# Sums of squares by TensorE, roots from products with ones and full-height low keys in a two-layer hybrid decoder step

## The chip, the core and the metric

The kernel runs on one core of a Trainium2 chip. A core has TensorE (PE, matrix products into PSUM), VectorE (DVE), ScalarE (ACT, functions from a table), GpSimd (POOL) and SyncE (SP, which here only issues DMAs); every engine works through its own queue in order. The metric is the time of one execution on the device in microseconds (us), median of several runs.

## What is computed

Two layers of a decoder step on a prompt of 1024 tokens and on 8 sequences of 4 new tokens; all 1056 tokens (T) share the weights. Cut to what matters here:

```python
mod = silu(c) @ w_ada + b_ada                     # shift, scale, gate
h = rms(x, g_pre) * (1 + scale) + shift           # rms: x * rsqrt(mean(x*x) + EPS) * g
u_a, bch, glu, q, k, v, mgate, mrg = split(h @ w_in)
y_a = pool_mixer(u_a); y_b = b_g * dwconv3(c_g * h_b)
y_c = silu(layernorm(dwconv31(val * sigmoid(gl))))
p = softmax(q k / 8) ; w = p[0] - lam * p[1]      # two maps per head, 64 deep each
y_d = rms(w @ v, g_subln) * (1 - lam_init)
merged = sum_n sigmoid(mrg_n) * (y_n * silu(mgate_n)) @ w_branch_n
x = x + gate * rms(merged @ w_o, g_post)
```

## The kernel before

Activations lie with channels on the 128 partitions and tokens along the row, in three column blocks `b` of TB = 352 tokens; the last 32 columns of block 2 are the sample tokens. Each product of float32 matrices is made of three products of rounded halves: `hh` and `hl` are the high and low part of the normed input, `whi` and `wlo` those of a weight tile, and `gemm` (line 238) issues `whi*hh`, `wlo*hh`, `whi*hl` for 8 slices `k` of 128 channels. A unit is 128 output channels: 24 products of 128x352 for each block. `drive` walks through the units, calls an evaluation function for each result, and between products it steps a second stream of work (`side`): the attention of a head (`attn`), the sample attention (`decode`) or the LayerNorm.

**Head.** Before the first unit, the program loads the input blocks `x0`, `x1`, `x2` (1408 KB each), the modulation weights `wa` (four slices `n` of four tiles, 512 KB each) and the first three weight tiles. `ada_first(n)` multiplies a slice with silu(c) (line 300), copies the result, transposes it (314) and adds the bias; slices 2 and 0 give scale and shift for the first four `k`, slices 3 and 1 for the others. `sumsq` (372 to 374) squares the input on ACT in two halves and adds the squares up on DVE; `rstd_x` makes the reciprocal root of it and broadcasts it to all partitions. `norm_apply` (L396 to L398) then makes `hh` and `hl`; for `k` in NORM_POOL it runs on POOL (391 to 394). The first products of blocks 0 and 1 use only `k` 0 to 3 (HALVES).

**Roots.** `rstd_of` sums over the partitions with products whose right side is one column of ones (349), so that the sums land on the partitions; ACT takes the square root (351), DVE the reciprocal (352), splits it in two rounded parts (355, 356) and writes each as a diagonal matrix (360); products with `ones` broadcast them (364). It is called twice at the end of each head's attention, 4 times by `decode`, 6 times by the LayerNorm, for each block behind the output projection, and for the next layer's input.

**Scores.** `a_part(qb)` makes the scores of 128 queries for one head: for each of the two maps `j` the products with the high keys and the mask, and then, for both maps together, the products with the low keys `kl`: map 0's low keys lie on partitions 0 to 63, map 1's on 64 to 127, and the products use 64 rows each.

A scheduler orders the instructions of every engine but SP from the order of the code and its own durations; SP's loads stand in the order of the code.

## Time and profile before

| what | us |
|---|---|
| median of 3 runs | 3004.43 (3002.55 to 3007.85) |
| profiled execution: its own time | 3002.23 |
| profiled execution: span of the core | 3000.4 |
| TensorE busy | 2913.8, 97% of the span |
| VectorE, ScalarE, GpSimd busy | 1634.2, 970.6, 495.1 |

The span is the profile's clock from the first to the last instruction; 1.8 us of the execution's own time lie outside it. Busy time of TensorE counts the time until a product has left the array, so that products overlap; what a product costs in a stream is the distance from its start to the start of the next one. The profile also gives the clock that was granted to TensorE: 1.0 is 2.4 GHz, 0.5 is 1.2 GHz.

### The profile page before, as it was taken

To read this page: it belongs to the slowest core of one execution; us is meant where nothing else is said; L and a number is where in the kernel's file an instruction comes from. 1 tells how busy PE (TensorE), PEld (TensorE's weight loads), DVE (VectorE), ACT (ScalarE), POOL (GpSimd) and SP (SyncE) were. 2 spreads that over 40 slices of the span, in tenths; PEclk is the share of its full clock that TensorE was granted. 3 is DMA by queue.
4 is the path that set the end of the run, shared out by engine and by line. 5 is a ranking of instruction groups with operands and counts; after the bars stand their busy time and mean duration, and the time that the engine had idled before them with its cause. 6 is when DMAs were issued, how large, how long until landed. Compare 5 with 4: busy or idle time off the path is not lost.

```text
span 3000.4 us, 46185 instructions
## 1 busy us (share of the span) xinstructions
PE 2913.8 (97%) x18436; PEld 2781.6 (93%) x18436; DVE 1634.2 (54%) x2540; ACT 970.6 (32%) x1904; POOL 495.1 (17%) x642
## 2 busy tenths in 40 slices
PE   6999999999999999999989999999999999999998
PEld 4899889989999999999989998998899999999998
DVE  7756356577972145323487663664889522543233
ACT  4544245313112123212454551542221121322132
POOL 3221011012200111011230120101140001110123
PEclk8999999999999999999999999999999999999999
DMA  6122621362233223222321236115511221221122
GB/s 230 48 65 85 203 78 53 116 196 64 67 109 105 80 86 96 97 75 71 108 98 48 67 118 205 49 45 153 179 38 59 84 76 43 80 90 57 50 69 97
DMA packets 135961, 280.08 MB, mean 93 GB/s; under 512 B 18338, under 2 KB 88994, under 8 KB 134210
## 3 DMA queue, kind: packets, MB, share of 16 engines
q10 hardware_dynamic: 45072, 145.74, 15.9%
q1 hardware_dynamic: 79778, 90.73, 9.7%
q0 software_dynamic: 10896, 40.67, 3.6%
q8 instruction: 145, 2.38, 0.3%
q14 instruction: 70, 0.57, 0.1%
HBM read 240.73 MB, written 36.34 MB: 92 GB/s over the span
## 4 chain that ended last, share of the span: by engine, by line
PE 84%; DVE 7%; DMA 2%; issue 2%; SPq 2%; ACT 2%; POOL 0%; DVEq 0%; ACTq 0%; POOLq 0%
PE mm_t L238 45%; PE m_t L238 28%; PE s_t L238 3%; PE ms_t L238 2%; DVE acc_t L954 2%; SPq L671 1%; PE ms_t L611 1%; PE s_t L776 1%; DVE wlo_t L211 1%; PE s_t L702 1%; DVE acc_t L373 1%; DMA e_t<-in_kc_dram 1%; PE ms_t L349 1%; PE b_t L238 1%; ACT rop_t L497 1%
## 5 line engine op out<-in xcount | busy, mean ns | idle before, releaser
L238 PE MATMUL mm_t<-hh_t,whi_t 128*128 128x352 f32 x2792 | 533.3, 329 | 5.8 <-ACT hh_t L385 2.1
L238 PE MATMUL mm_t<-hh_t,wlo_t 128*128 128x352 f32 x2792 | 528.6, 327 | 0.0
L238 PE MATMUL mm_t<-hl_t,whi_t 128*128 128x352 f32 x2792 | 524.0, 325 | 0.0
L211 DVE TENSOR_TENSOR wlo_t<-wst_t,whi_t 128x1024 fp32r<-128x1024 f32 x203 | 268.5, 1329 | 455.6 <-ACT whi_t L210 455.4
L238 PEld LDWEIGHTS mm_t<-hh_t,whi_t 128*128 128x128 f32 x2792 | 458.7, 190 | 27.6 <-issue 14.6
L238 PEld LDWEIGHTS mm_t<-hh_t,wlo_t 128*128 128x128 f32 x2792 | 460.5, 189 | 9.7 <-issue 8.2
L238 PEld LDWEIGHTS mm_t<-hl_t,whi_t 128*128 128x128 f32 x2792 | 458.7, 189 | 6.7 <-issue 5.6
L954 DVE SCALAR_TENSOR_TENSOR acc_t<-uc_t,vec_t,acc_t 128x1024 f32<-128x1024 f32 x240 | 320.4, 1360 | 1.6
L1164 POOL TENSOR_TENSOR mg_t<-mg_t,th_t 128x352 f32<-128x352 f32 x144 | 144.7, 1008 | 925.8 <-DVE th_t L1163 925.7
L210 ACT ACTIVATE whi_t<-wst_t 128x1024 fp32r<-128x1024 f32 x203 | 213.3, 1056 | 246.7 <-PE mm_t L238 163.6
L238 PE MATMUL m_t<-hh_t,wlo_t 128*128 128x352 f32 x1352 | 249.7, 325 | 0.0
L238 PE MATMUL m_t<-hl_t,whi_t 128*128 128x352 f32 x1352 | 247.6, 324 | 0.0
L238 PE MATMUL m_t<-hh_t,whi_t 128*128 128x352 f32 x1352 | 246.4, 323 | 0.0
L238 PEld LDWEIGHTS m_t<-hh_t,wlo_t 128*128 128x128 f32 x1352 | 223.6, 190 | 0.9
L238 PEld LDWEIGHTS m_t<-hl_t,whi_t 128*128 128x128 f32 x1352 | 222.7, 189 | 0.0
L238 PEld LDWEIGHTS m_t<-hh_t,whi_t 128*128 128x128 f32 x1352 | 222.0, 189 | 0.1
L1072 ACT ACTIVATE th_t<-m_t 128x352 f32<-128x352 f32 x114 | 52.6, 463 | 373.4 <-PE m_t L238 362.5
L1072 ACT ACTIVATE th_t<-mm_t 128x352 f32<-128x352 f32 x78 | 35.9, 463 | 272.0 <-PE mm_t L238 240.9
L590 DVE TENSOR_REDUCE sml_t<-s_t 128x1 f32<-128x256 f32 (+7 forms) x128 | 92.4, 752 | 53.1 <-PE s_t L238 52.7
L593 ACT ACTIVATE e_t<-s_t,sml_t 128x256 f32<-128x256 f32 (+7 forms) x128 | 94.3, 744 | 69.7 <-DVE sml_t L591 39.9
L238 PE MATMUL m_t<-yh_t,whi_t 128*128 128x352 f32 x460 | 94.5, 326 | 0.0
L238 PE MATMUL m_t<-yh_t,wlo_t 128*128 128x352 f32 x460 | 93.1, 324 | 0.0
(349 smaller groups left out, 3854.0 us busy)
## 6 DMA issues: line engine op xcount, KB each, us to landing
wst_t<-in_wst_dram ACTq DMA_DIRECT2D x209, 512.0 KB, 3.6
e_t<-in_kc_dram SPq DMA_DIRECT2D x224, 128.0 KB, 3.0
e_t<-in_vc_dram SPq DMA_DIRECT2D x216, 128.0 KB, 2.6
rld_t<-ysp_t ACTq DMA_DIRECT2D x16, 528.0 KB, 4.5
wa_t<-in_wada_dram SPq DMA_DIRECT2D x16, 512.0 KB, 10.4
wlo_t<-in_wada_dram ACTq DMA_DIRECT2D x16, 512.0 KB, 3.7
whi_t<-in_wada_dram ACTq DMA_DIRECT2D x16, 512.0 KB, 4.3
x_t<-in_xT_dram SPq DMA_DIRECT2D x3, 1408.0 KB, 6.0
```

Of the source, the lines that this page charges most:

```text
L210: sc.activation(out=R(hi), in_=st, func=AF.Copy)
L211: (eng or ve).tensor_tensor(out=R(lo), in0=st, in1=hi, op=ALU.subtract)
L238: last_mm[0] = m = te.matmul(out=out, lhsT=R(lh), rhs=R(rh), start=first and i == 0, stop=last and i == n - 1)
L349: te.matmul(out=pc[:, j:j + 1], lhsT=x[:, j * w:(j + 1) * w], rhs=ones[:, 0:1], start=True, stop=True)
L373: ve.tensor_reduce(out=acc[:, i], in_=o.rearrange("p k n -> p n k"), axis=AX.X, op=ALU.add)
L497: sc.activation(out=sw[32 * (g ^ 1):32 * (g ^ 1) + 32], in_=pb[32 * g:32 * g + 32], func=AF.Copy)
L590: ve.tensor_reduce(out=s[:, j:j + 1], in_=S[j][:, :n], axis=AX.X, op=ALU.max)
L593: sc.activation(out=E[qb % 2][j][:, :n], in_=S[j][:, :n], func=AF.Exp, bias=s[:, 2 + j:3 + j], scale=0.125, accum_out=s[:, 4 + j:5 + j])
L611: te.transpose(out=pb[:, k], in_=e0[:, (k0 + k) * P:(k0 + k + 1) * P], identity=ident)
L954: pace(ve.scalar_tensor_tensor(out=a, in0=v, scalar=w(k), in1=a, op0=ALU.mult, op1=ALU.add))
L1072: sc.activation(out=th[:, b * TB:(b + 1) * TB], in_=pb, func=AF.Tanh, scale=0.5)
L1164: gp.tensor_tensor(out=mg[:, d, cl], in0=mg[:, d, cl], in1=th, op=ALU.add)
```

## The change

Of the head: the order of loads becomes `x0`, slices 0 and 2, the weight tiles, `x1`, slices 1 and 3, `x2` (before `x0`, `x1`, slices 0 and 2, weight tiles, `x2`, slices 1 and 3). The sums of squares are no longer added on DVE: eight float32 products with `ones` (128x352 each) add the squares up and broadcast them in one step. POOL has no part in the modulation of the first layer any more, except for the sample columns. Block 1's first half now comes before slices 1 and 3.

Of the roots: `rstd_of` splits its input in two rounded parts (ACT, DVE), two products with `ones` sum and broadcast it, and ACT and DVE then make the reciprocal root on all columns, with one correction step (4 operations on 128 x 352 or 512 elements). The factor -2 that the correction leaves is put into constants and into the operations that use the root.

Of the scores: the queries of a block are copied into `qz` with zeros in the other 64 rows (two copies on ACT), so that the products with the low keys use all 128 rows; they follow the high keys of their own map, and the pairing of the two maps falls away.

```diff
-    def rstd_of(x, n, scale, dg, pb=None):
-        w = max(w_ for w_ in (P, TB // 4, 64) if n % w_ == 0)
-        m = n // w
-        pc = ms(m)[:w]
-        for j in range(m):
-            te.matmul(out=pc[:, j:j + 1], lhsT=x[:, j * w:(j + 1) * w], rhs=ones[:, 0:1], start=True, stop=True)
-        r = const("rsm", 8, bufs=2)[:w, 0:m]
-        sc.activation(out=r, in_=pc, func=AF.Sqrt, bias=epsc[:w], scale=scale)
-        ve.reciprocal(out=r, in_=r)
...
-        for i, d in enumerate(dg):
-            te.matmul(out=pb, lhsT=cast(ones[:w]), rhs=cast(d[:w]), start=i == 0, stop=i == len(dg) - 1)
+    def rstd_of(x, scale, parts, yt, pb=None):
+        if parts:
+            hi, lo = parts
+            sc.activation(out=R(hi), in_=x, func=AF.Copy, scale=scale)
+            ve.scalar_tensor_tensor(out=R(lo), in0=x, scalar=scale, in1=hi, op0=ALU.mult, op1=ALU.subtract)
+            for i in range(2):
+                te.matmul(out=pb, lhsT=R(ones), rhs=R(parts[i]), start=i == 0, stop=i == 1)
+        else:
+            te.matmul(out=pb, lhsT=ones, rhs=x, start=True, stop=True)
...
+        sc.activation(out=y, in_=pb, func=AF.Abs_reciprocal_sqrt, bias=epsc)
+        sc.activation(out=t, in_=y, func=AF.Square)
+        ve.scalar_tensor_tensor(out=pb, in0=pb, scalar=EPS, in1=t, op0=ALU.add, op1=ALU.mult)
+        ve.scalar_tensor_tensor(out=pb, in0=pb, scalar=-3.0, in1=y, op0=ALU.add, op1=ALU.mult)
...
                 for j in range(2):
-                    for c0, w in chunks:
-                        c = slice(c0, c0 + max(w, 256))
+                    r = slice(64 * j, 64 * j + 64)
+                    sc.activation(out=R(qz[r, qb % 2, j]), in_=qs[j][r, q1], func=AF.Copy)
+                for j in range(2):
+                    for c in chunks:
                         gemm(S[j][:, c], [(qs[j][:, q1], ks[j][:, c])], last=False)
-                    gemm(S[j][:, q1], [(identr, maskr)], first=False, last=False)
+                        if c is chunks[-1]:
+                            gemm(S[j][:, q1], [(identr, maskr)], first=False, last=False)
+                        gemm(S[j][:, c], [(qz[:, qb % 2, j], kl[:, c])], first=False)
                     if j == 0:
                         yield
-                hi = last_mm[0]
-                for c0, w in chunks:
-                    c = slice(c0, c0 + max(w, 256))
-                    for j in range(2):
-                        r = slice(64 * j, 64 * j + 64)
-                        gemm(S[j][:, c], [(qs[j][r, q1], kl[r, c])], first=False, on=hi)
...
         def rstd_x(b):
-            a = accs[b]
-            pb = rstd_of(a[:, 0], TB, 1.0 / D, [a[:, 1]])
-            sc.activation(out=a[:, 0], in_=pb, func=AF.Copy)
-        for b in range(2):
-            sp.dma_start(out=xb0[b], in_=xT[b])
+            t, y = two(accs[b])
+            pb = ms(TB)
+            for i in range(2):
+                tx = su("tx", 4, TB, bufs=2)
+                sc.activation(out=tx, in_=xb0[b][:, 4 * i:4 * i + 4], func=AF.Square)
+                for k in range(4):
+                    te.matmul(out=pb, lhsT=ones, rhs=tx[:, k], start=i + k == 0, stop=i + k == 4)
...
+        sp.dma_start(out=xb0[0], in_=xT[0])
...
+        sp.dma_start(out=xb0[1], in_=xT[1])
         ada_first(2, psA("mm", 512))
...
+        first_half(0)
+        rstd_x(1)
+        first_half(1)
+        for n in (1, 3):
+            ada_first(n, ms())
+        make_A(0, 4, 4)
+        rstd_x(2)
```

How this moves the instructions on TensorE, at three places. `cs_t` holds the identity of a transpose, `m_t` a copied modulation slice, `tx_t` the squared input, `acc_t` the sums before.

The first instructions of TensorE, before:

```order
L300 MATMUL mm_t<-wa_t,scs_t 32x512 x8
L314 MATMUL ms_t<-cs_t,m_t 128x128 x4
L349 MATMUL ms_t<-ones_t,acc_t 88x1 x4
L300 MATMUL mm_t<-wa_t,scs_t 32x512 x4
L364 MATMUL ms_t<-acc_t,ones_t 128x352
L349 MATMUL ms_t<-ones_t,acc_t 88x1 x4
L300 MATMUL mm_t<-wa_t,scs_t 32x512 x4
L364 MATMUL ms_t<-acc_t,ones_t 128x352
L314 MATMUL ms_t<-cs_t,m_t 128x128 x4
L238 MATMUL b_t<-hh_t,whi_t 128x352 x3
```

and now:

```order
L1260 MATMUL ms_t<-tx_t,ones_t 128x352 x4
L298 MATMUL mm_t<-wa_t,scs_t 32x512 x2
L1260 MATMUL ms_t<-tx_t,ones_t 128x352 x4
L298 MATMUL mm_t<-wa_t,scs_t 32x512 x10
L312 MATMUL ms_t<-cs_t,m_t 128x128 x4
L298 MATMUL mm_t<-wa_t,scs_t 32x512 x4
L312 MATMUL ms_t<-cs_t,m_t 128x128 x4
```

The eight products for block 0's squares now stand ahead of almost all modulation products, and the root of block 1 is gone from the place ahead of the first unit.

The end of the first head's attention on TensorE (from the last products with the values, `vl_t`, to the last product with `ones`), before:

```order
L238 MATMUL ms_t<-e_t,vl_t 128x256
L349 MATMUL ms_t<-ones_t,ms_t 128x1 x4
L238 MATMUL mm_t<-hh_t,whi_t 128x352 x6
L238 MATMUL mm_t<-hh_t,wlo_t 128x352 x8
L238 MATMUL mm_t<-hl_t,whi_t 128x352 x8
L238 MATMUL mm_t<-hh_t,whi_t 128x352 x8
L364 MATMUL ms_t<-e_t,ones_t 128x512
L349 MATMUL ms_t<-ones_t,ms_t 128x1 x2
L364 MATMUL ms_t<-e_t,ones_t 128x512
L349 MATMUL ms_t<-ones_t,ms_t 128x1 x2
L238 MATMUL mm_t<-hh_t,wlo_t 128x352 x8
```

and now:

```order
L236 MATMUL ms_t<-e_t,vl_t 128x256
L236 MATMUL mm_t<-hh_t,wlo_t 128x352
L236 MATMUL mm_t<-hl_t,whi_t 128x352 x8
L236 MATMUL mm_t<-hh_t,whi_t 128x352 x6
L354 MATMUL ms_t<-e_t,ones_t 128x512
L236 MATMUL mm_t<-hh_t,whi_t 128x352 x2
L236 MATMUL mm_t<-hh_t,wlo_t 128x352 x3
L354 MATMUL ms_t<-e_t,ones_t 128x512
L236 MATMUL mm_t<-hh_t,wlo_t 128x352 x5
L236 MATMUL mm_t<-hl_t,whi_t 128x352 x5
L354 MATMUL ms_t<-e_t,ones_t 128x512
```

The one-column products are gone; between the last products with the values and the first product with `ones` stand 15 products of units.

The scores of a block of 768 keys on TensorE, first head before (`kl_t` the low keys, `maskr_t` the mask):

```order
L238 MATMUL s_t<-k_t,q_t 128x512
L238 MATMUL s_t<-k_t,q_t 128x256
L238 MATMUL s_t<-maskr_t,identr_t 128x128
L238 MATMUL mm_t<-hh_t,whi_t 128x352 x2
L238 MATMUL s_t<-k_t,q_t 128x512
L238 MATMUL s_t<-k_t,q_t 128x256
L238 MATMUL s_t<-maskr_t,identr_t 128x128
L238 MATMUL s_t<-kl_t,q_t 128x512 x2
L238 MATMUL s_t<-kl_t,q_t 128x256 x2
```

and now, third head (`ms_t` is the tile of `qz`):

```order
L236 MATMUL s_t<-k_t,q_t 128x512
L236 MATMUL s_t<-kl_t,ms_t 128x512
L236 MATMUL s_t<-k_t,q_t 128x256
L236 MATMUL s_t<-maskr_t,identr_t 128x128
L236 MATMUL s_t<-kl_t,ms_t 128x256
L236 MATMUL s_t<-k_t,q_t 128x512
L236 MATMUL s_t<-kl_t,ms_t 128x512
L236 MATMUL s_t<-k_t,q_t 128x256
L236 MATMUL s_t<-maskr_t,identr_t 128x128
L236 MATMUL s_t<-kl_t,ms_t 128x256
```

Each map's low keys have moved up to its own high keys, chunk by chunk, ahead of the other map's products.

## Rows read from the trace of the kernel before

**Rows 1.** The page, part 1: busy us, share of the span, instructions.

```profile
PE 2913.8 (97%) x18436; PEld 2781.6 (93%) x18436; DVE 1634.2 (54%) x2540; ACT 970.6 (32%) x1904; POOL 495.1 (17%) x642
```

**Rows 2.** The page, part 4: the chain that ended last, by engine.

```profile
PE 84%; DVE 7%; DMA 2%; issue 2%; SPq 2%; ACT 2%; POOL 0%; DVEq 0%; ACTq 0%; POOLq 0%
```

**Rows 3.** Chain of the first 80 us, in order: start, us, what.

```profile
1.21 5.97 DMA x_t<-in_xT_dram
...
8.61 2.55 DVE acc_t L373
...
36.46 1.25 PE b_t L238 x3
```

**Rows 4.** Stretches: us; engines' busy time (instructions); PEclk, DMA share, GB/s.

```profile
20.00:36.00 16.00, 10.78 (x44) 5.73 (x44) 11.64 (x24) 7.29 (x12) 4.28 (x5) 0.53 1.02 412
...
78.00:82.00 4.00, 3.56 (x13) 3.56 (x14) 2.98 (x8) 2.64 (x5) 3.97 (x13) 0.50 0.12 45
```

**Rows 5.** Timeline, TensorE, head: start, us, line, out<-in, shape, [idle before <-who].

```profile
25.40 1.51 PE L364 MATMUL ms_t<-acc_t,ones_t 88*128 88x352 f32 x2 [0.27 <-DVE acc_t L360]
26.70 1.24 PE L349 MATMUL ms_t<-ones_t,acc_t 128*88 128x1 f32 x8
...
29.84 1.51 PE L364 MATMUL ms_t<-acc_t,ones_t 88*128 88x352 f32 x2
...
51.76 1.92 PE L300 MATMUL ms_t<-wa_t,scs_t 128*32 128x512 f32 x16
...
60.45 0.76 PE L364 MATMUL ms_t<-acc_t,ones_t 88*128 88x352 f32 x2
...
78.44 0.90 PE L526 MATMUL ms_t<-cs_t,vcm_t 128*128 128x128 f32 x3 [6.07 <-ACT vcm_t L541]
```

**Rows 6.** Timeline, ScalarE: first and last of the chain ahead of 78.44.

```profile
68.26 0.92 ACT L497 ACTIVATE rop_t<-b_t 32x352 f32<-32x352 f32 x2
...
77.92 0.46 ACT L541 ACTIVATE vcm_t<-mm_t 128x352 f32<-128x352 f32 x1
```

**Rows 7.** Groups of VectorE: modulation with GpSimd beside it, and without (layer 1).

```profile
L396 DVE SCALAR_TENSOR_TENSOR x_t<-x_t,Am_t,acc_t 128x352 f32<-128x352 f32 x12 | 8.5, 768 | 0.0
...
L396 DVE SCALAR_TENSOR_TENSOR ob_t<-xb_t,Am_t,ms_t 128x352 f32<-128x352 f32 x16 | 8.1, 577 | 7.0 <-PE ms_t L364 7.0
```

**Rows 8.** One-column products: timeline of one call, then groups from 100 us on.

```profile
162.70 0.95 PE L349 MATMUL ms_t<-ones_t,ms_t 128*128 128x1 f32 x8
163.51 1.22 PE L238 MATMUL mm_t<-hh_t,whi_t 128*128 128x352 f32 x6
...
L349 PE MATMUL ms_t<-ones_t,ms_t x128: 164/250/250, 162.7 to 2053.1; 128*128 128x1 f32 x128
L349 PE MATMUL ms_t<-ones_t,ls_t x48: 164/217/217, 1105.0 to 2655.3; 128*88 128x1 f32 x48
```

**Rows 9.** Timeline, TensorE: scores of a block of 1024 and of 256 keys.

```profile
252.63 0.63 PE L238 MATMUL s_t<-k_t,q_t 128*128 128x512 f32 x2
253.10 0.22 PE L238 MATMUL s_t<-maskr_t,identr_t 128*128 128x128 f32 x1
253.25 0.73 PE L238 MATMUL s_t<-kl_t,q_t 64*128 64x512 f32 x4
253.91 0.51 PE L238 MATMUL ms_t<-e_t,vh_t 128*128 128x256 f32 x2
...
201.41 0.38 PE L238 MATMUL s_t<-kl_t,q_t 64*128 64x256 f32 x2
201.73 0.76 PE L238 MATMUL mm_t<-hh_t,whi_t 128*128 128x352 f32 x3
```

**Rows 10.** Timeline of the end: the last root.

```profile
2985.74 0.52 DVE L1211 TENSOR_TENSOR ssq_t<-ssq_t,sq_t 128x352 f32<-128x352 f32 x1
2986.32 0.79 PE L349 MATMUL ms_t<-ones_t,ssq_t 128*88 128x1 f32 x8 [1.69 <-DVE ssq_t L1211]
...
2989.62 0.89 DVE L1219 TENSOR_TENSOR ob_t<-ob_t,ada_t 128x704 f32<-128x704 f32 x1 [0.75 <-PE ada_t L364]
```

More of the change, by code (lines that the diff above doesn't have):

```diff
@@ L375, in sumsq, with norm_apply @@
         return acc[:, 0]
-    def norm_apply(l, b, x, t, rs, hh, hl, pool=(), ks=range(KC)):
+    def norm_apply(l, b, x, t, rs, hh, hl, ks=range(KC)):
         n = npr(b)
@@ L644, in attn @@
                 c = slice(i * 512, i * 512 + 512)
-                dg = ep(f"e{i}", 1024)
-                rs = rstd_of(msq[:, c], 512, 1.0 / P, two(dg.rearrange("p (i n) -> p i n", i=2)))
+                dg, yt = [ep(f"e{i + x}", 1024).rearrange("p (i n) -> p i n", i=2) for x in (0, 2)]
+                msq = ep(f"e{4 + i}", 1024)[:, 0:512]
+                sc.activation(out=msq, in_=o[:, c], func=AF.Square)
+                rs = rstd_of(msq, 1.0 / P, two(dg), two(yt))
                 ve.tensor_tensor(out=o[:, c], in0=o[:, c], in1=rs, op=ALU.mult)
@@ L1096, in layernorm @@
                 yield from skip(6)
-                rs = rstd_of(s2, TB, 1.0 / 512, [lnp("ls1", TB), lnp("ls3", TB)])
-                ve.tensor_tensor(out=x, in0=x, in1=rs.unsqueeze(1).to_broadcast([P, 4, TB]), op=ALU.mult)
+                rs = rstd_of(s2, 1.0 / 512, [lnp(f"lr{i}", TB) for i in range(2)], [t[:, i] for i in range(2)])
+                ve.scalar_tensor_tensor(out=x, in0=rs.unsqueeze(1).to_broadcast([P, 4, TB]), scalar=-0.5, in1=x,
+                                        op0=ALU.mult, op1=ALU.mult)
                 for c in range(4):
@@ L1215, in layer @@
                 ve.tensor_tensor(out=scols(ob[:, :, n:]), in0=scols(ob[:, :, n:]), in1=samp(GG), op=ALU.mult)
-            rs = rstd_of(ssq, TB, 1.0 / D, two(op("acc", 2, TB)), psM("ada", 512)[:, 0:TB])
+            rs = rstd_of(ssq, 1.0 / D, two(op("parts", 2, TB)), two(op("yt", 2, TB)), psM("ada", 512)[:, 0:TB])
             for d in range(0, KC, 2):
                 o_, x_ = ob[:, d:d + 2], xb[:, d:d + 2]
-                ve.tensor_tensor(out=o_, in0=o_, in1=rs.unsqueeze(1).to_broadcast([P, 2, TB]), op=ALU.mult)
+                ve.scalar_tensor_tensor(out=o_, in0=rs.unsqueeze(1).to_broadcast([P, 2, TB]), scalar=-0.5, in1=o_,
+                                        op0=ALU.mult, op1=ALU.mult)
                 (gp if d % 4 else ve).tensor_tensor(out=x_, in0=x_, in1=o_, op=ALU.add)
@@ L1222, in layer @@
                 gp.dma_start(out=xmid[b], in_=xb)
-                rs = rstd_of(sumsq(xb, ob, op("acc", 2, TB)), TB, 1.0 / D, two(op("acc", 2, TB)))
+                rs = rstd_of(sumsq(xb, ob, op("acc", 2, TB)), 1.0 / D, two(op("parts", 2, TB)), two(op("yt", 2, TB)))
                 for t, x in zip(nh, "hl"):
```

69 lines of the change are left out of this document (26 added, 43 removed).

## The prediction

> **What bounds the kernel now.** I read the page first: TensorE is busy for 97% of the span, no other engine for more than 54% [rows 1], and 84% of the chain that ended last is TensorE's own work [rows 2]. So what counts is what leaves TensorE's queue, and the few places where that queue stands still. The chain of the first 80 us shows the largest of them, the head: the first unit product starts at 36.46 [rows 3], behind a chain of squares on ACT and sums on DVE. In the timeline there is one more wait of 6.07 us that ends at 78.44 [rows 5]. Loads are no shorter than this: between 20 and 36 us the DMA engines are full, at 412 GB/s [rows 4].
>
> **The head.** Block 0 of the input lands at 1.21 + 5.97 = 7.2 and its first square is done at 8.6 [rows 3]. Removed are the sums on DVE (six of 2.55, the first in [rows 3]) that paced the squares; added are eight float32 products for each block. Their price has two ends. At a granted clock of 0.5 such a product takes 26.70 - 25.40 = 1.30; at full clock it is half, 0.65, as its busy time shows (1.51 against 0.76) [rows 5]. The granted clock was 0.53 between 20 and 36 [rows 4], where TensorE had waits between short products. The new queue begins with full-height products of 352 columns one behind the other from 8.6 on; I take the full clock from some 15 us on, and keep the half clock as a rival.
>
> Slice 2 decides when the first unit can start. x1 (1408 KB, 1.44 MB) now lies behind it: 3.5 us at 412 GB/s. By bytes (x0 at 7.2, then 6.0 MB) slice 2 landed at 21.9 and now lands at 18.4. By then TensorE has done block 0's eight products (some 8.6 to 16, slice 0 between them, part of it at half clock) and gets through slice 2 at 20.8. Before, 36.46 - 31.14 = 5.3 passed from the end of the last root products (29.84 + 1.30) [rows 5] to the first unit product [rows 3]. With the copy ahead of it (0.6) that gives 20.8 + 0.6 + 5.3 = 26.7. That POOL no longer works beside DVE makes a modulation 577 instead of 768 ns [rows 7], against two more for each half block: a wash, taken as nothing.
>
> From there on everything is in TensorE's queue. A product of 352 columns costs 0.162, since 1024 columns took 253.10 - 252.63 = 0.47 [rows 9]. Half of block 0 is 36 of them, 5.9, and 6.4 as DVE has to write the low parts: 33.1. Block 1's eight: 5.2, 38.3. Slices 1 and 3 land by then; their 16 products cost 2 x 1.92 [rows 5] and 0.6 for transposes: 42.7. Half of block 1: 48.6. Transposes 0.6 and block 2's eight, 5.2: 54.4. Block 2 itself lands last of all loads, near 40, and waits for nobody. The first unit of block 0 is finished after 38 further products: 60.6. Then TensorE runs into the wait that it has today: ScalarE needs from 68.26 to 78.38 to take away the units and to make block 2's high parts [rows 6], 10.1 us, and the change leaves that list as long as it was. So the wait ends at 70.7 instead of 78.4: **-7.5**. The bound on the good side is -9, with full clock from the first product. If half clock holds until the first unit product, this starts at 32.8, the following pieces move with it, and the wait ends near 79.7: +1.3.
>
> **The roots.** A call of `rstd_of` loses its one-column products: eight records at the end of attention cost TensorE 163.51 - 162.70 = 0.81 [rows 8]. The products with `ones` that broadcast stay, two for each call, with the same columns. Per layer there are 8 calls in attention, so 16: -13.0. With 88 instead of 128 columns of weights a call is put at 88/128 of that, 0.56; 15 such calls lie behind the head: 6 of the LayerNorm (48 records of eight a call [rows 8]), 6 behind the output projection, 3 for the next layer's input. Three of them end in a wait of TensorE for the chain anyway (the last of all, two at the layer boundary), so 12: -6.7. Four calls of the sample attention have two records each: -0.8. Sum **-20.5**, all of it in stretches where TensorE is the bound.
>
> What is added lies on ACT and DVE: for each call a copy, a root and a square on ACT and three operations on DVE, on 352 or 512 columns, instead of short ones on 4 columns and two diagonals. That is nothing where TensorE has other products queued: 15 of them (2.4 us) stand between the last products with the values and the first with `ones`. At two places there is no cover. At the end, before: from 2986.32 to 2989.62, 3.3 [rows 10]. Now a copy 0.46, a difference 0.52, the products 0.6, root and square 2 x 0.46, two corrections 2 x 0.52, and some 0.3 between them: 3.9 (0.46 is a 352-column copy on ACT [rows 6], 0.52 a 352-column operation on DVE [rows 10]). **+0.6**, and **+0.6** again at the layer boundary, where the first unit of block 2 waits for the second root.
>
> The root now also keeps one of the two PSUM tiles of its kind for some 4 us longer, and table loads on ACT fall into that time; transposes of the next head need such a tile. Today TensorE does not wait there; I take 0, and up to 1.5 for each of the 8 heads, +12, for the range.
>
> **The low keys.** Before, a block of 1024 keys occupies TensorE from the mask at 253.10 to the next product at 253.91, 0.81, of which the mask's 128 columns are 0.06: 0.75. With all rows in use it is 2 x 0.47 = 0.94 [rows 9]. For 256 keys it was 253.25 - 253.10 - 0.06 + 201.73 - 201.41 = 0.41, and will be 2 x 0.12. So the paired products do run beside each other, but each time 0.3 is lost when they begin and end. Over the eight blocks of a head (256 twice, 384, 512, 768 twice, 896, 1024 columns, 4864 in all, the middle ones by the same two parts) it is 4.53 before and 4864 x 0.47 / 1024 = 4.47 after: **-0.5** for 8 heads.
>
> The Trainium skill speaks against this edit: "TensorEngine Tiling (Array Packing)", Theoretical Speedup, promises a speedup where a contraction of at most 64 rows is packed as several tiles that work at once. By that rule alone the edit gives up the whole gain of the pairs, 17.9 in all as in rival 3. The row for 256 keys speaks against it: 0.41 is more than the 0.24 of the single file.
>
> The two copies of queries for each block are 128 instructions on ACT, at about 0.3 each 35 us of an engine that is 32% busy; in ACT's order they stand right behind the queries' own split, well ahead of the scores. Taken as 0. Decode's first cache loads wait for the root's tiles; the second diagonal came late (its column sums stood behind the first root), now both halves run closer together, while two more tiles are held a little longer. Taken as 0, with -6 as the bound.
>
> **The sum.** -7.5 - 20.5 + 0.6 + 0.6 - 0.5 = -27.3. From the profiled execution's 3002.2 this is 2974.9; that execution lay 2.2 under the median of 3004.4, so I predict 2977.
>
> **Rivals.** (1) *Half clock in the head*: +1.3 instead of -7.5, 2986. For it: 0.53 between 20 and 36 with TensorE two thirds busy [rows 4]; against: those were products of 32 or one column. Chance 0.17. (2) *Roots become waits*: PSUM tiles or table loads stop TensorE at the heads' ends, +12: 2989. Against: half of ACT and DVE is free. 0.12. (3) *The loss at entry and exit stays*: if the 0.3 per block belongs to the change between high and low keys and not to the pairs, the new form has it too, and a head gives up half of its 4.47, 2.24; for 8 heads that is +17.9 in place of -0.5: 2977 + 18.4 = 2995. For it: no product with low keys on 128 rows is in the trace; against: high keys follow each other without such a loss [rows 9]. 0.06. (4) *Slower*: TensorE waits at each product with low keys for the copy of the queries, because ACT has it behind an exponential or an evacuation. 128 such products, each behind one ACT operation of 0.46 [rows 6] and the wait for it, 0.5 together: +64, 3041. It decides from 27.3 / 128 = 0.21 per product on. Against it: queries are ready long before, and two blocks are held. 0.03. That the edit of the column sums does not take place is out: the one-column products are gone from the order.
>
> **How the numbers follow.** The forecast's own case has 0.62 and spans 2964 to 2984 (from -6 for the loads, -1.5 for the head and a part of the waits, to some waits). The range of 2962 to 2989 takes in the first two rivals. A measurement of this kernel tells about 0.2%, 6 us, from no change. Faster by more: 0.62 + 0.17 + 0.12 + most of 0.06, 0.94; within: 0.03; slower: 0.03.
>
> **What would show it.** Head right: TensorE's first unit product near 26.7, the wait for ScalarE ends near 71; wrong: PEclk 0.5 up to the first unit product, or a new wait at slices 1 and 3. Roots right: no group of one-column products, and the LayerNorm and output stretches shorter by 0.56 for each call; wrong: waits of TensorE for the root's tiles at heads' ends. Low keys right: scores as long as before within 1 us a head, no wait for the copies. End right: 0.6 longer from the last sum to the first multiplication.

## The result

| kernel | median, us | range | runs |
|---|---|---|---|
| before | 3003.49 | 3001.87 to 3007.85 | 4 |
| changed | 2973.56 | 2970.82 to 2977.08 | 4 |

The ratio is 0.9899, with a 95% interval of 0.9882 to 0.9916: 29.9 us less, where the prediction had 2977 and a range of 2962 to 2989. The profiled execution of the changed kernel took 2971.34, its span is 2969.6, against 3000.4 before.

### The profile after

The page of the changed kernel, parts 1 and 4 (as [rows 1, 2]):

```profile
PE 2882.3 (97%) x18198; PEld 2774.0 (93%) x18198; DVE 1618.5 (55%) x2488; ACT 1060.0 (36%) x2086; POOL 483.1 (16%) x632
...
PE 80%; DVE 7%; ACT 5%; DMA 3%; SPq 3%; issue 2%; POOL 0%; ACTq 0%; DVEq 0%; POOLq 0%
```

TensorE is the bound as before. 238 products less were recorded; ScalarE is busy for 89 us more and has grown from 2% to 5% of the chain that ended last. That is the first hint of what the list of waits shows (changed kernel, TensorE; columns: product and line, waited for, us in total, times, longest):

```profile
PE s_t L236 <- ACT e_t L585: 11.3, 8, 3.2
PE ms_t L236 <- ACT dh_t L1014: 9.4, 2, 5.3
...
PE ms_t L354 <- ACT parts_t L351: 7.9, 2, 7.7
PE mm_t L236 <- ACT hh_t L383: 4.8, 1, 4.8
PE ms_t L518 <- ACT vcm_t L533: 4.4, 1, 4.4
...
PE ada_t L354 <- ACT parts_t L351: 2.2, 1, 2.2
PE ms_t L1084 <- DVE ls_t L1081: 2.0, 3, 1.1
```

The first row is new: at eight places score products wait for exponentials. The waits of decode for its cache loads fell from 12.9 to 8.0 (the two stretches of `decode` in the lists of both kernels).

Places of the program that both kernels have, with their starts in the two timelines, split the gain into stages. The last column is the prediction's sum for the stage.

| up to | before | changed | stage | predicted |
|---|---|---|---|---|
| first score product | 84.40 | 78.01 | -6.4 | -7.5 |
| first merge step of layer 1 on GpSimd (`mg_t`) | 964.45 | 948.54 | -9.5 | -7.2 |
| first product with `woh_t`, layer 1 | 1439.49 | 1420.80 | -2.8 | -1.7 |
| first merge step of layer 2 | 2445.45 | 2416.10 | -10.7 | -8.8 |
| first product with `woh_t`, layer 2 | 2900.82 | 2871.56 | +0.1 | -1.7 |
| end of the span | 3000.4 | 2969.6 | -1.5 | -0.5 |

The sum is close, -30.8 against -27.4, but two stages with attention won more than forecast although they have a new wait. So some terms must be wrong in both directions.

### The profile page after: what moved, and what is told of

Read it like the earlier page. It is cut to its first block, busy times and chain, and to the rows that moved or that the text cites. A ratio compares the mean times of both kernels' runs of the same rounds, so it can differ in the third digit from the quotient of the medians.

```text
span 2969.6 us, 45889 instructions
## 1 busy us (share of the span) xinstructions
PE 2882.3 (97%) x18198; PEld 2774.0 (93%) x18198; DVE 1618.5 (55%) x2488; ACT 1060.0 (36%) x2086; POOL 483.1 (16%) x632
## 4 chain that ended last, share of the span: by engine, by line
PE 80%; DVE 7%; ACT 5%; DMA 3%; SPq 3%; issue 2%; POOL 0%; ACTq 0%; DVEq 0%; POOLq 0%
PE mm_t L236 42%; PE m_t L236 28%; PE s_t L236 3%; DVE acc_t L947 2%; SPq L664 2%; PE ms_t L236 2%; PE ms_t L603 1%; DMA e_t<-in_kc_dram 1%; ACT rop_t L489 1%; SPq L401 1%; DVE wlo_t L209 1%; PE s_t L769 1%; PE s_t L695 1%; PE ada_t L298 1%; PE ms_t L1260 1%
## 5 line engine op out<-in xcount | busy, mean ns | idle before, releaser
L585 ACT ACTIVATE e_t<-s_t,sml_t 128x256 f32<-128x256 f32 (+7 forms) x128 | 94.2, 739 | 51.7 <-DVE sml_t L583 50.7
L236 PE MATMUL m_t<-yl_t,whi_t 128*128 128x352 f32 x460 | 93.2, 324 | 0.0
## 6 DMA issues: line engine op xcount, KB each, us to landing
x_t<-in_xT_dram SPq DMA_DIRECT2D x3, 1408.0 KB, 12.9
```

What stands on the lines that cost most here:

```text
L236: last_mm[0] = m = te.matmul(out=out, lhsT=R(lh), rhs=R(rh), start=first and i == 0, stop=last and i == n - 1)
L585: sc.activation(out=E[qb % 2][j][:, :n], in_=S[j][:, :n], func=AF.Exp, bias=s[:, 2 + j:3 + j], scale=0.125, accum_out=s[:, 4 + j:5 + j])
```

## The experiments

Twelve kernels were run, each beside runs of the kernel before on the same chip. These had medians of 3003.36 (first four), 3003.89 (next four), 3002.32 (next three) and 3003.25 (last). The changed kernel itself was not run again beside them, so differences to it compare sets of runs. All single runs of e3, e4, f4 and g2 lie above the changed kernel's 2970.8 to 2977.1, and all of f1 below; those of f2, f3, g3 and h1 lie within it or overlap it, so that for these only the profiles can tell a difference. f3, f4 and g3 were run twice each.

| run | median | ratio to before | 95% interval |
|---|---|---|---|
| e1 head alone | 2993.30 | 0.9966 | 0.9951 to 0.9980 |
| e2 roots alone | 2984.54 | 0.9936 | 0.9915 to 0.9956 |
| e3 changed, low keys as before | 2981.54 | 0.9921 | 0.9905 to 0.9938 |
| e4 changed, roots as before | 2987.81 | 0.9937 | 0.9919 to 0.9954 |
| f1 changed, exponentials behind the root | 2964.77 | 0.9877 | 0.9861 to 0.9894 |
| f2 changed, four slots for queries | 2976.96 | 0.9908 | 0.9891 to 0.9924 |
| f3 changed, loads as before | 2971.86 | 0.9895 | 0.9875 to 0.9915 |
| f4 changed, GpSimd back in the modulation | 2980.18 | 0.9923 | 0.9903 to 0.9943 |
| g1 before, GpSimd out of the modulation | 2999.15 | 0.9985 | 0.9975 to 0.9996 |
| g2 changed, low keys in 64 rows, single | 3017.66 | 1.0050 | 1.0036 to 1.0064 |
| g3 changed, sums of squares by VectorE | 2973.05 | 0.9901 | 0.9872 to 0.9930 |
| h1 changed, head's squares and roots as before | 2978.13 | 0.9926 | 0.9907 to 0.9944 |

### Which part brought what: e1 to e4

e1 is the kernel before with the head of the change (the factor -2 is put into `make_A` for layer 0 alone); e2 is the kernel before with the new `rstd_of`, its callers and constants; e3 and e4 are the changed kernel with one part taken back.

e1:

```diff
+        if l == 0:
+            ve.tensor_scalar(out=a, in0=a, scalar1=-0.5, scalar2=None, op0=ALU.mult)
...
-        for b in range(2):
-            sp.dma_start(out=xb0[b], in_=xT[b])
...
+                for k in range(4):
+                    te.matmul(out=pb, lhsT=ones, rhs=tx[:, k], start=i + k == 0, stop=i + k == 4)
...
+        sp.dma_start(out=xb0[0], in_=xT[0])
```

> The kernel before with the changed head alone (order of loads, sums of squares by TensorE, no GpSimd in the first modulation); roots and low keys as before. Theory: the head is worth what its rows say, the wait for ScalarE ends near 71.0 instead of 78.4, of which a longer stretch at half clock behind it takes 1.0 back; nothing later gives it back: 3003.5 - 6.4 = 2997, 2995 to 2999. Rival: the waits of decode for its cache loads (some 13 us in all before) do not start earlier with the head and swallow the gain: 3003, with these waits longer than before by 4 to 6.

Measured: 10 less, a little past the good end of the expectation. In the profile the scores start at 78.46, and from there to the end of layer 1 most places are 6.6 to 9.0 earlier than before (6.74 from 1200 to 1500 us), so the gain of the head isn't given back there. In layer 2 it is 3.8 to 5.6 between 1800 and 2000 us and 9.8 at the end: behind 2000 us TensorE's waits sum to 12.6 where before they sum to 15.9. So some 3 of the 10 are not the head's own. The rival with decode's loads falls.

e2:

```diff
-    def rstd_of(x, n, scale, dg, pb=None):
+    def rstd_of(x, scale, parts, yt, pb=None):
...
+            for i in range(2):
+                te.matmul(out=pb, lhsT=R(ones), rhs=R(parts[i]), start=i == 0, stop=i == 1)
...
+        sc.activation(out=y, in_=pb, func=AF.Abs_reciprocal_sqrt, bias=epsc)
+        sc.activation(out=t, in_=y, func=AF.Square)
...
+    def rstd_old(x, n, scale, dg, pb=None):
```

> The kernel before with the changed roots alone; head and low keys as before (the head keeps the old root). Theory: 20.5 of one-column products gone, the waits of TensorE for the scores' exponentials at 467 to 480 and 1930 to 1945 come from the roots' table loads on ScalarE (four of 1.28 in 10 us), so they show here too, 5 in each layer: 2983 to 2988. Rival: those waits come from the copies of queries, which this kernel has not: 2981 or less, no wait of a score product for an exponential.

Measured: 18.8 less, as the prediction had it for the roots (-20.5 + 1.2 = -19.3), and the wait for an exponential is there without any copy of queries. Its row (waits of TensorE, e2, 400 to 500 us):

```profile
PE s_t L238 <- ACT e_t L618: 3.2, 1, 3.2
```

The kernel before has no wait at all in that stretch. In both layers together these waits are 6.4, against 11.3 in the changed kernel. A part of the agreement in size is luck: in the two LayerNorm stages e2 gains some 2.8 more than the changed kernel; its unit products take 161.0 ns each there instead of 161.5, and no term of the prediction holds that.

e3:

```diff
-                    for c in chunks:
+                    for c0, w in chunks:
+                        c = slice(c0, c0 + max(w, 256))
                         gemm(S[j][:, c], [(qs[j][:, q1], ks[j][:, c])], last=False)
-                        if c is chunks[-1]:
-                            gemm(S[j][:, q1], [(identr, maskr)], first=False, last=False)
-                        gemm(S[j][:, c], [(qz[:, qb % 2, j], kl[:, c])], first=False)
+                    gemm(S[j][:, q1], [(identr, maskr)], first=False, last=False)
...
+                hi = last_mm[0]
+                for c0, w in chunks:
+                    c = slice(c0, c0 + max(w, 256))
+                    for j in range(2):
+                        r = slice(64 * j, 64 * j + 64)
+                        gemm(S[j][:, c], [(qs[j][r, q1], kl[r, c])], first=False, on=hi)
```

> The changed kernel with the low keys as before (pairs of 64 rows, no copies of queries). Theory by the prediction: pairs and full height cost the same within 1, the waits of score products for exponentials stay, since table loads make them: 2973 to 2977. Rival: the copies stand in ScalarE's queue and wait there for earlier scores, and the exponentials behind them are late by that; without copies the waits (5.6 in each layer and the half clock behind them) go, against 1.5 a layer that the paired products cost: 2961 to 2966.

Measured: 2981.5, 8 more than the changed kernel and outside both expectations. The wait at the exponentials is smaller here (3.2 in each layer instead of 5.6), and yet the kernel is slower: the pairs cost far more than the prediction thought.

e4:

```diff
+        ve.tensor_scalar(out=r, in0=r, scalar1=-2.0, scalar2=None, op0=ALU.mult)
...
-            for i in range(2):
-                te.matmul(out=pb, lhsT=R(ones), rhs=R(parts[i]), start=i == 0, stop=i == 1)
...
+        for i, d in enumerate(dg):
+            te.matmul(out=pb, lhsT=cast(ones[:w]), rhs=cast(d[:w]), start=i == 0, stop=i == len(dg) - 1)
```

> The changed kernel with the roots made as before (one-column products, root on 4 columns, diagonals; one more small multiplication by -2 on VectorE); head and low keys stay changed. Theory: the roots are worth what the one-column products cost: 2973.5 + 20 = 2993, 2990 to 2997, and the waits of score products for exponentials go. Rival: the waits stay, then they are the copies'; and if part of the gain lay in decode's loads, these waits come back: up to 2999.

Measured: 2987.8, under the expected 2990 to 2997. The roots are worth 14 in this company by the medians and 19 by the two profiled spans (2988.7 and 2969.6), so the runs leave open whether that is less than alone. The waits for exponentials shrink to 0.6 in 400 to 500 us (and 1.2 for a product that waits for a copy), so with the copies of queries alone they are nearly gone: the new roots make them, the copies add to them.

The parts do not simply add up. Head and roots gain 10.1 and 18.8 alone (e1, e2); e3, which has both, gains 21.8. On top of the roots the head is thus worth 3.0 by the medians and some 1 by the two profiles, although it still brings the scores 5.9 forward. A part of the difference is e2's lower price of unit products; the rest wasn't traced.

### What the low keys cost: e3 against the changed kernel, and g2

For layer 1's attention, from the first score product to the first merge step, I added up for each kind of product the distance from its start to the next start (waits over 0.2 apart). All in us:

| | before | e2 | e3 | changed | f1 | g2 |
|---|---|---|---|---|---|---|
| high keys | 18.0 | 18.7 | 18.8 | 19.2 | 19.1 | 25.6 |
| mask | 7.4 | 7.6 | 7.7 | 4.0 | 4.5 | 9.7 |
| low keys | 19.1 | 19.1 | 19.1 | 21.2 | 21.5 | 36.3 |
| products of units | 713.1 | 715.5 | 716.5 | 710.0 | 708.9 | 713.9 |
| products with values | 30.1 | 29.7 | 29.7 | 28.4 | 28.4 | 29.1 |
| sums with `ones` | 12.1 | 4.0 | 4.0 | 4.0 | 4.0 | 4.0 |
| transposes, decode, rest | 64.8 | 65.3 | 65.3 | 66.0 | 66.3 | 64.4 |
| waits | 15.5 | 14.7 | 14.7 | 17.7 | 13.3 | 12.9 |
| sum | 880.1 | 874.6 | 875.8 | 870.5 | 865.9 | 895.9 |

From e3 to the changed kernel the low keys themselves cost 2.1 more, as products of full height in single file. But the mask ahead of them costs 3.7 less, the values 1.3 less and the units 6.5 less. Of the latter, 3.2 are the unit product right behind a pair (30 of them, 0.11 too long each). The rest is mostly a second stretch at half clock that e3 has and the changed kernel has not: from 567 to 575 us the granted clock was 0.57 in e3, behind waits in the sample attention, and 1.00 in the changed kernel from 560 to 575. The stretch at half clock behind the wait for the exponentials is as long in both, 6.8. The timeline of a block of 1024 keys in the changed kernel, first map, then second, and of unit products behind an ordinary product:

```profile
230.40 0.65 PE L236 MATMUL mm_t<-hh_t,wlo_t 128*128 128x352 f32 x3
...
238.41 0.39 PE L236 MATMUL s_t<-k_t,q_t 128*128 128x512 f32 x1
238.63 0.39 PE L236 MATMUL s_t<-kl_t,ms_t 128*128 128x512 f32 x1
238.87 0.39 PE L236 MATMUL s_t<-k_t,q_t 128*128 128x512 f32 x1
239.10 0.22 PE L236 MATMUL s_t<-maskr_t,identr_t 128*128 128x128 f32 x1
239.15 0.44 PE L236 MATMUL s_t<-kl_t,ms_t 128*128 128x512 f32 x1
239.44 0.48 PE L236 MATMUL mm_t<-hl_t,whi_t 128*128 128x352 f32 x2
```

High and low keys follow each other at 0.22 to 0.24, and the mask takes 0.05; in [rows 9] it was 0.15. The loss at the other end was in [rows 9] too, one row further than I looked: behind the pairs, three unit products take 0.76 instead of 0.65 here, and the two products with the values 0.51. Rival (3), that high and low keys lose time next to each other also at full height, falls by these rows.

g2 asks whether the pairing or the 64 rows cost that:

```diff
-                        gemm(S[j][:, c], [(qz[:, qb % 2, j], kl[:, c])], first=False)
+                        r = slice(64 * j, 64 * j + 64)
+                        gemm(S[j][:, c], [(qs[j][r, q1], kl[r, c])], first=False)
```

> The changed kernel, in which the low keys are multiplied in 64 rows again, without copies of queries, but in the changed order: each map's behind its own high keys, not paired. Theory: the loss at entry (mask 0.05 more) and exit (0.105 on the next unit product) that the pairs showed belongs to each change between 128 and 64 rows; there are now two to four such groups for a block instead of one, the columns go in single file: 2973.6 + 15 to 25, 2988 to 2999. Rival: the loss belongs to two groups of 64 rows side by side; single products of 64 rows cost what those of 128 rows cost: 2970 to 2974, and the copies were needless.

Measured: 3017.7, 44 more than the changed kernel: in the direction of the theory, but far outside its range. The same block in g2:

```profile
253.49 0.40 PE L236 MATMUL s_t<-k_t,q_t 128*128 128x512 f32 x1
253.82 0.50 PE L236 MATMUL s_t<-kl_t,q_t 64*128 64x512 f32 x1
254.25 0.50 PE L236 MATMUL s_t<-k_t,q_t 128*128 128x512 f32 x1
254.59 0.22 PE L236 MATMUL s_t<-maskr_t,identr_t 128*128 128x128 f32 x1
254.74 0.50 PE L236 MATMUL s_t<-kl_t,q_t 64*128 64x512 f32 x1
255.17 0.59 PE L236 MATMUL mm_t<-hl_t,whi_t 128*128 128x352 f32 x2
```

Start to start, the product ahead of 64 rows takes 0.33 (0.10 more), that with 64 rows 0.43 (0.19 more), and the one behind it 0.34 (0.11 more). So the pairing isn't needed for the loss: every change of height costs here. From the changed kernel to g2, high keys +6.4, mask +5.7, low keys +15.1 and units +3.9 make 31.1 for 96 visits to 64 rows in the layer, 0.32 each. The Trainium skill, "TensorEngine Tiling (Array Packing)", Key Properties, says that changing the tiling mode drains TensorE; that fits these rows, and the page gives no size for it.

### The wait for the exponentials: f1 and f2

ScalarE of the changed kernel between 463 and 474 us, at the change from the third to the fourth head (L359 is the root, L585 the exponential):

```profile
463.39 1.28 ACT L359 ACT_TABLE_LOAD   x1
464.69 0.69 ACT L359 ACTIVATE e_t<-ms_t,epsc_t 128x512 f32<-128x512 f32 x1
...
465.59 1.28 ACT L585 ACT_TABLE_LOAD   x1
466.88 0.37 ACT L585 ACTIVATE e_t<-s_t,sml_t 128x128 f32<-128x128 f32 x1
...
468.21 1.28 ACT L359 ACT_TABLE_LOAD   x1
...
471.83 1.28 ACT L585 ACT_TABLE_LOAD   x1
473.12 0.37 ACT L585 ACTIVATE e_t<-s_t,sml_t 128x128 f32<-128x128 f32 x1
```

Root, exponential, root, exponential: four table loads, and only at 473.49 is the score tile free that TensorE waits for (3.20 us, up to 473.63). f1 lets the first exponentials of a head follow the second root of the head before:

```diff
+                    if qb == 0 and last_rt[0] is not None:
+                        pace(ex, last_rt[0])
```

> The changed kernel, in which the first exponentials of a head stand behind the second root of the head before in ScalarE's order (8 table loads less in all). Theory: the waits of score products for exponentials (5.6 in each layer, with a stretch at half clock behind them) come from the two switches of tables between the two roots of a head and the first exponentials of the next; without them the second exponential of the block ends some 3 earlier, the waits shrink to 2 or less in each layer: 2973.6 - 7 = 2966, 2963 to 2969. Rival: the exponentials are late for ScalarE's and VectorE's other work of the root (squares, parts, corrections) and now also for the later place: waits as before or longer, 2973 to 2979.

Measured: 2964.8, 8.8 less than the changed kernel. The intervals of the two ratios overlap, but the single runs, 2961.6 to 2970.0, lie below those of the changed kernel, and the profiles place the difference. ScalarE in f1, same place:

```profile
461.50 1.28 ACT L359 ACT_TABLE_LOAD   x1
...
464.56 0.69 ACT L359 ACTIVATE e_t<-ms_t,epsc_t 128x512 f32<-128x512 f32 x1
...
466.37 1.28 ACT L585 ACT_TABLE_LOAD   x1
467.67 0.37 ACT L585 ACTIVATE e_t<-s_t,sml_t 128x128 f32<-128x128 f32 x1
...
468.54 0.36 ACT L585 ACTIVATE e_t<-s_t,sml_t 128x128 f32<-128x128 f32 x1
```

From the root's table load to the end of the second exponential it is 7.4 instead of 10.1. The 2.7 between them are two loads of 1.28. In the whole kernel 42 table loads are left of 50, and the waits for exponentials fell from 11.3 to 3.0 (a new one of 3.7 for `od_t` beside them). By the two profiles f1 gains 4.8 between 350 and 700 us, and 9.8 by the end. Of these, 0.9 arise ahead of the attention, before any head's root, and some 2.5 in layer 2's attention; the part that lies outside these waits wasn't traced. Not all of the wait comes from the alternation: e2 has none at that place, and in it the first exponential stands at 481 behind rotations, a weight split and one table load. The Trainium skill, "ScalarE: Activation LUTs", Table sets, asks to batch activations by set; f1 is that rule. Its section What ACT_TABLE_LOAD costs has about 1283 ns for the load, which the 1.28 of these rows agree with, and about 2.66 us for a whole switch, which they don't: in the changed kernel it is 1.31 from the end of the operation before (465.57) to the exponential (466.88), and the measurement decides. This is the fastest kernel of the study.

f2 gives the copied queries four slots and copies for two blocks at once:

```diff
-                    sc.activation(out=R(qz[r, qb % 2, j]), in_=qs[j][r, q1], func=AF.Copy)
+                if qb % 2 == 0 or qb == 5:
+                    w2 = P if qb in (4, 5) else 2 * P
...
+                        sc.activation(out=R(qz[r, j, q0 % 512:q0 % 512 + w2]), in_=qs[j][r, q0:q0 + w2], func=AF.Copy)
```

> The changed kernel with four slots for the copied queries instead of two, and the copies of two blocks made at once (80 instead of 128 of them). Theory: the copies cost nothing but ScalarE's time, except between 476 and 481 and at the like place of layer 2, where a copy waits 1.31 and 0.68 for an earlier score product that reads its slot, and exponentials stand behind it: that goes, 2 to 4 in all, 2970 to 2972. Rival: the copies were hidden there too, and only the order shifts: 2972 to 2975.

Measured: 2977.0, no gain, and beyond both expectations. The scheduler put the instructions in another order (46 table loads, roots and exponentials still alternating), and in place of the wait came others:

```profile
PE ms_t L518 <- DVE sml_t L585: 8.1, 2, 4.2
...
PE s_t L236 <- ACT e_t L587: 5.8, 2, 2.9
```

That leaves the price of the copies open: a kernel that changes only them, and not the order, wasn't tried.

### What the head's gain hangs on: f3, f4, g1, g3, h1

The head came out as predicted. Timeline of TensorE in the changed kernel:

```profile
9.11 4.16 PE L1260 MATMUL ms_t<-tx_t,ones_t 128*128 128x352 f32 x8 [9.11 <-ACT tx_t L1258]
...
14.18 2.63 PE L1260 MATMUL ms_t<-tx_t,ones_t 128*128 128x352 f32 x8
...
25.88 3.72 PE L236 MATMUL b_t<-hh_t,whi_t 128*128 128x352 f32 x10 [3.32 <-ACT hh_t L389]
...
33.60 4.89 PE L1260 MATMUL ms_t<-tx_t,ones_t 128*128 128x352 f32 x16
...
49.83 4.90 PE L1260 MATMUL ms_t<-tx_t,ones_t 128*128 128x352 f32 x16
54.30 2.03 PE L236 MATMUL b_t<-hh_t,whi_t 128*128 128x352 f32 x10
...
70.99 0.90 PE L518 MATMUL ms_t<-cs_t,vcm_t 128*128 128x128 f32 x3 [4.44 <-ACT vcm_t L533]
```

But its causes were tested one by one. f3 takes the loads back to their old order:

```diff
         sp.dma_start(out=xb0[0], in_=xT[0])
+        sp.dma_start(out=xb0[1], in_=xT[1])
...
-        sp.dma_start(out=xb0[1], in_=xT[1])
...
+        sp.dma_start(out=xb0[2], in_=xT[2])
         ada_load(1)
         ada_load(3)
-        sp.dma_start(out=xb0[2], in_=xT[2])
```

> The changed kernel with the loads of the head in the order of before (block 1 ahead of the modulation weights, block 2 ahead of slices 1 and 3). Theory: slice 2 lands 3.5 later by its bytes, the first unit product starts near 29.4 instead of 25.9, and TensorE's queue behind it moves with it; the wait for ScalarE ends at 74 to 74.5: 2977. Rival: TensorE is not late for slice 2, since block 0's squares and the short products before it set the time, or the loads of slices 1 and 3 do: first unit product before 27, 2974; or slices 1 and 3 come late behind block 2 too: wait near 42, 2979.

Measured: 2971.9, no loss. Slice 2 is late as expected, and the first unit product starts at 29.15, 3.3 later and close to the 29.4 expected, yet the wait ends where it did, as neither expectation had it:

```profile
24.62 4.90 PE L1260 MATMUL ms_t<-tx_t,ones_t 128*128 128x352 f32 x16
29.15 0.85 PE L236 MATMUL b_t<-hh_t,whi_t 128*128 128x352 f32 x3
...
71.03 0.90 PE L518 MATMUL ms_t<-cs_t,vcm_t 128*128 128x128 f32 x3 [4.44 <-ACT vcm_t L533]
```

The scheduler had put block 1's squares, which had landed, ahead of the first unit (24.62 to 29.5). Here the products that must be done anyway cost nothing earlier.

g3 has the squares added up by VectorE again, and TensorE only sums over the partitions:

```diff
-                for k in range(4):
-                    te.matmul(out=pb, lhsT=ones, rhs=tx[:, k], start=i + k == 0, stop=i + k == 4)
+                ve.tensor_reduce(out=accs[b][:, i], in_=tx.rearrange("p k n -> p n k"), axis=AX.X, op=ALU.add)
+                te.matmul(out=pb, lhsT=ones, rhs=accs[b][:, i], start=i == 0, stop=i == 1)
```

> The changed kernel, in which VectorE adds up the squares of four k again (2.55 each, six of them) and TensorE only sums over the partitions (two float32 products for each block instead of eight). Theory: TensorE is the bound from 25.9 to 66, so 18 products of 0.65 less, 11.7, come off its queue, but the wait for ScalarE behind it then grows, since its list (10 us) starts with the first finished units: the wait ends at 67 to 70, 2969 to 2973. Rival: VectorE is late with the sums or, for them, with the modulations; TensorE waits in the half blocks, the wait ends at 73 to 77: 2976 to 2980.

Measured: 2973.1, the same. The wait ends earlier and what follows waits longer (TensorE, g3):

```profile
68.12 0.90 PE L518 MATMUL ms_t<-cs_t,vcm_t 128*128 128x128 f32 x3 [5.00 <-ACT vcm_t L533]
70.05 2.71 PE L236 MATMUL mm_t<-hh_t,whi_t 128*128 128x352 f32 x8 [1.02 <-ACT hh_t L383]
...
77.77 0.35 PE L236 MATMUL s_t<-k_t,q_t 128*128 128x256 f32 x1 [1.22 <-DVE q_t L501]
```

The scores start at 77.77 against 78.01: ScalarE and VectorE set the end of the head, not TensorE's list.

f4 gives GpSimd `k` 2 and 4 again, g1 takes them away in the kernel before:

```diff
-            norm_apply(0, b, xb0[b], xb0[b], accs[b][:, 0], h[0][b], h[1][b], HALVES[0])
+            norm_apply(0, b, xb0[b], xb0[b], accs[b][:, 0], h[0][b], h[1][b], (2, 4), HALVES[0])
```

> The changed kernel, in which GpSimd again does the first modulation for k 2 and 4. Theory: a wash, as the prediction took it: GpSimd's part ends by 29, its low parts are wanted near 31, and VectorE's modulations go back from 577 to some 770 ns; wait for ScalarE ends within 1 of 71.0, 2972 to 2976. Rival: GpSimd's low parts are late in block 0 or block 1 and TensorE waits for them: the wait for ScalarE moves by 2 or more, 2976 to 2979.

Measured: 2980.2, 6.6 more, just past the rival's range. In the profile the scores start at 84.28, where they started before the change, and from 200 us on nearly all places are 8.0 to 9.4 later than in the changed kernel. The rival is right that TensorE waits (TensorE, f4):

```profile
27.66 3.85 PE L236 MATMUL b_t<-hh_t,whi_t 128*128 128x352 f32 x10 [4.06 <-ACT hh_t L395]
...
49.37 0.96 PE L236 MATMUL b_t<-hh_t,whi_t 128*128 128x352 f32 x2 [2.59 <-ACT hh_t L391]
```

But not all of it is GpSimd's pace. The second wait is for ScalarE's copy of a slice that GpSimd had finished at 46.29; in ScalarE's order that copy stands behind block 2's squares (46.31, 2.62 us).

```diff
-NORM_POOL = (2, 4)
+NORM_POOL = ()
```

> The kernel before, in which GpSimd has no part in the first modulation (its list of k is empty; the sample columns stay with it), and nothing else changed. Theory after the run with GpSimd put back (8.5 later from the head on): GpSimd's share is what costs, and the gain of the head alone (6.7) is this one edit: 2995 to 2998, the wait for ScalarE ends by 72. Rival: in the old head the squares, their sums on VectorE and the roots set the time up to 36, two more modulations fall to a VectorE that is full there, and little is won: 3001 to 3005; then it is TensorE's sums that made room on VectorE.

Measured: 2999.2, 3.2 less, between the two expectations. Up to 300 us the places are only 1.6 earlier; from there into layer 2 they are level with before within 0.7, and from 2200 us on some 3 earlier. Taken alone, the edit is worth little: the first unit still starts at 35.76, behind the old roots, and the scores at 83.87 against 84.40. Once these roots are gone, giving GpSimd its share back costs 6.6 by the medians.

h1 keeps the new order of code and loads and leaves GpSimd out, but makes squares, sums and roots of the head as before:

```diff
+            sumsq(xb0[b], tx, a)
+            pb = rstd_old(a[:, 0], TB, 1.0 / D, [a[:, 1]])
+            sc.activation(out=a[:, 0], in_=pb, func=AF.Copy, scale=-2.0)
```

> The changed kernel with the head's squares, sums and roots made as before (sums on VectorE, one-column products, diagonals), but the changed order of code and loads, and no GpSimd in the modulation. After the runs that left loads and sums without effect, 5 of the head's 6.7 are open: order of the code (block 1's root and first half behind block 0's) or form of the root. Theory, order: slice 2's products no longer stand behind block 1's root in TensorE's queue, the first unit product starts near 26, and VectorE has room for the old sums there as in the run with its sums: scores begin near 78, 2972 to 2976. Rival, form: the one-column products and diagonals make TensorE wait in the head again, the scores begin at 82 to 83, 2977 to 2981.

Measured: 2978.1, in the rival's range, though the lowest runs (2976.9 and 2977.4) meet the highest of the changed kernel. The profile shows the rival more strongly than expected at the scores (TensorE, h1):

```profile
29.72 3.63 PE L236 MATMUL b_t<-hh_t,whi_t 128*128 128x352 f32 x10 [4.36 <-ACT hh_t L414]
...
38.98 0.76 PE L372 MATMUL ms_t<-ones_t,acc_t 128*88 128x1 f32 x8 [1.43 <-DVE acc_t L397]
40.94 1.51 PE L387 MATMUL ms_t<-acc_t,ones_t 88*128 88x352 f32 x2 [1.21 <-DVE acc_t L383]
...
82.54 0.90 PE L543 MATMUL ms_t<-cs_t,vcm_t 128*128 128x128 f32 x3 [3.58 <-ACT vcm_t L558]
89.10 0.28 PE L236 MATMUL s_t<-k_t,q_t 128*128 128x256 f32 x1
```

The scores start at 89.10, 11 later and later even than before the change (84.40). Since g3 shows VectorE's sums to be harmless, the head's gain hangs on the form of the root (no one-column products, no diagonals, no second trip through TensorE) together with GpSimd's absence. One thing keeps this from being fully shown: h1 also has only one buffer for the squares again, where the changed kernel and g3 have two, and no run parts that from the root. Of the 11.8 at 700 us 7.2 are left at the end of the span. That loss is gradual and goes on where TensorE has no waits (between 1000 and 1400 us a unit product takes 161.0 ns in h1 and 161.5 in the changed kernel); its cause stays open.

## Why the prediction was right, and where only its sum was

**The bound.** Right: TensorE stays at 97%, and what left its queue left the time.

**The head: right size, partly wrong reason.** The steps came out one after the other: first unit product 26.7 predicted, 25.88 measured; block 1's eight 33.1, 33.60; block 2's eight end at 54.4, 54.30; the wait ends at 70.7, 70.99. Rival (1) fell: full clock by 14.18, four products in 2.6, with a short half-clock stretch behind 25.88 (ten unit products in 3.72). What failed is the sentence that from the first unit on everything follows in TensorE's queue, and the 3.5 of the loads: f3 shows that the first unit may start 3.3 later for nothing. The wash that I took for GpSimd holds for VectorE's busy time (16.6 in the changed kernel, 16.1 in f4), but not for the queues: f4 is 6.6 slower. One piece I had not counted: behind the wait the 24 products up to the scores took 71.55 to 78.01, 6.5, where before they took 79.00 to 84.40, 5.4. The stretch at half clock is 6.8 in both, but 6.1 of it now lie behind the wait, where it was 3.9; so 7.4 became 6.4.

**The roots.** Right in size and place: predicted -19.3, e2 -18.8. In the attention of layer 1 the sums with `ones` fell from 12.1 to 4.0, 8.1 where the prediction had 6.5 + 0.4. The LayerNorm gave -2.7 in both layers instead of -3.4. In layer 1 one-column products (1.7) and waits (2.6) are gone, but the modulation products took 1.9 more; in layer 2 the one-column products are gone (1.7), but the wait for the row sums ahead of it grew from 0.4 to 1.8. The tail's +0.6 came out as +0.5: from the end of the last sum to the multiplication it is 2954.90 to 2958.76, 3.9 (3.4 from 2986.26 in [rows 10]).

```profile
2954.38 0.52 DVE L1205 TENSOR_TENSOR ssq_t<-ssq_t,sq_t 128x352 f32<-128x352 f32 x1
...
2958.76 3.28 DVE L1213 SCALAR_TENSOR_TENSOR ob_t<-ada_t,ob_t 128x704 f32<-128x704 f32 x4
```

**The low keys: the mis-sized term.** -0.5 predicted; 8 by the medians of e3 and the changed kernel. The step that failed is the price of a pair: I measured from the mask to the start of the next product, and a delay that a product hands on shows only in the distance from its successor's start to the one after. That is 0.105 at each of the 80 exits from pairs that the trace of before has, 8 in all, which the prediction missed. In layer 1 mask and low keys together also fell by 1.6 (e3 to the changed kernel), where the sum had 0.25; against both stand the changed kernel's longer waits for exponentials, 11.3 where e3 has 6.4.

**The waits that were taken as 0.** Rival (2) happened in part: 5.6 in each layer and the half clock behind it, though not for PSUM tiles but for exponentials behind the root's table loads and its other work on ScalarE. f1, which keeps roots and exponentials apart, is 8.8 faster, though not all of that lies in these waits. Decode's loads gave some 5 (bound -6, taken as 0). So that the forecast was met this closely is luck in part: a gain of 8 that it did not see and a gain of 5 at decode stood against waits that it had only in the range.

**The boundary between the layers.** Taken as +0.6; there the waits grew (5.7 for `acc_t` and 2.1 for `hh_t` before, 7.7 for `parts_t` and 4.8 for `hh_t` now). From the first product with `woh_t` of layer 1 to the first score product of layer 2 TensorE took 111.8 before (1439.49 to 1551.33) and takes 108.3 now (1420.80 to 1529.11): 3.1 less of one-column products and 0.6 less of waits. Behind it some 1.5 are given back in the waits for block 2, so the boundary gained about 2. The 1.9 by which the stage that holds it beat the forecast therefore lie in layer 2's attention.

## What to carry to other kernels

Read the price of a product from the start of the one before it to the start of the second one behind it: TensorE hands delays on, and a change between heights of 64 and 128 rows cost a third of a microsecond at each visit here. When ScalarE gets a new function, look at what stands beside it in ScalarE's order: the busy share (36%) says nothing, and an order that keeps two functions from different tables apart at a few places was 8.8 us faster by the medians of f1 and the changed kernel, if not for that reason alone. And a stage whose parts were each tested alone may still be misjudged: GpSimd's share cost 3.2 by the medians beside the old roots (g1) and 6.6 beside the new ones (f4).

## What was unexpected in the hardware

Products of 64 rows between products of 128 rows: 0.10 more on the product ahead, 0.19 on itself and 0.11 on the one behind (g2), so that the halved time of a pair is eaten up at these sizes; at 128 rows the same change of operands costs nothing in the rows above. And the first float32 products of 352 columns cost double: 1.17 each from 9.11 to 12.2 us (two records of 0.59) and 0.59 from 12.5 us on. That this was the clock is inferred from the price alone, since the granted clock of the profile is 1.00 in that stretch.
